# Joins of a group's banks at set times inside the next group, and four pairs by seven products in attention's output

## The chip, the cores and the metric

The kernel runs on one core of a Trainium2 chip. The metric is the device time of one execution in microseconds, as the median of several executions. A profiled execution of the same kernel gives the trace; its time and its span are listed below.

## The reference

One layer of a hybrid decoder trunk is computed in float32 for 256 tokens and a model width of 2048. Cut to what matters:

```python
h = rmsnorm(x, g_mix)
x_r, g_r, q, k, v, gate_r, gate_a = split(h @ w_in)
y_r = (gelu(g_r) * rg_lru(conv1d(x_r), w_rg_a, ..., lru_lambda)) @ w_rnn_out
q, k = head_rmsnorm(q), head_rmsnorm(k)          # 16 heads of 128
y_a = stick_breaking_attention(q, k, v) @ w_attn_out
mix = sigmoid(gate_r) * y_r + sigmoid(gate_a) * y_a
x = x + mix @ w_o
g, u = split(rmsnorm(x, g_ffn) @ w_ffn_gu)
x = x + (silu(g) * u) @ w_ffn_down
ple_gate = sigmoid(rmsnorm(x, g_ple) @ w_ple_gate)
out = x + ple_gate * (p @ w_ple_proj)
```

Nearly all of the work is in the matrix products with the weights, and each weight is read once.

## The kernel before

**Numbers in two parts.** Every operand of a product is kept as a high and a low part of reduced precision, and a product is three matmuls: high by high, high by low, low by high. In `prod` they are lines L645, L646 and L647, each 128 x 128 by 128 x 512.

**The stream of weights.** Weights come in chunks of 128 x 1024. SP's queue loads them (L284), 512 KB each, into tiles `w` or, where sums of weights are needed, `Q`. A split then makes the two parts: ScalarE copies the high part (`whi`, L373) and VectorE subtracts it (`wlo`, L374). The class `Stream` issues the splits four chunks ahead of the products (`need`), and sums two chunks further.

**Seven products for eight.** Most stages are run by `group`. A group makes four blocks of output, two blocks of 128 tokens by two halves of columns of 512. Two k-tiles taken as a pair form a 2 by 2 product that a Winograd scheme makes in seven products instead of eight. For this the weights are combined: VectorE adds (`summed`, L295), and GpSimd issues DMAs that accumulate a second weight chunk onto a tile in SBUF (`joins`, L333). The activations are combined once per pair by `half_sums`. A list of slots says in which order chunks are used: `FIRST3` and `EVEN3` have three pairs and ten plain k-tiles, `EVEN4` and `LONG` have four pairs, `TWELVE` has two pairs. `FOUR` names the stages with four pairs; `pairs_of` reads it.

**Banks.** PSUM has a pool of eight banks (`pps`). A group accumulates into six of them, named B, 5, 2, 4, 3 and 8 after their part in the scheme. B and 5 are copied out by ScalarE during the group. When the group has ended, `whole` adds each of the other four to a copied tile on VectorE: these four adds are the joins, `tt(c, q, c, ALU.add)` (L453, `H<-ps`). They give their banks back to the pool. `wo`, `dn` and `pg` have joins of their own, which add a bank onto the residual stream (`x1`) or to the gate.

**Order.** The stages are, in order: recurrent gates and branch, then `ro`, `v`, `qk` (two groups each), dense blocks of q, k and gates with attention in steps between them (`step`), `ao` (attention's output), `wo`, `gu` 0 to 3, `dn0`, `gu` 4 to 7, `dn1`, `gu` 8 to 10, `dn2`, `pg`. There are 28 places where one group follows another. The order of instructions on each engine is planned by the scheduler of the Tile framework, which simulates a timeline; `tc.issue_after` adds constraints. `behind_splits` makes what is issued in it stand behind the last split's two instructions.

Work on a group's results that is not the join itself (multiplying by a gate, the heads' norms, silu) goes to a list `todo`, of which one item is run at the start of each slot of the next group or each step of a block. Pieces that transpose results on TensorE for the next stage are in `pend`; one is run at each of the slots in `TURNED_AT`, if `todo` gave nothing to that slot. `squares` makes the sums of squares for the norms with ScalarE, `token_scales` the scales from them.

Of the kernel before, what the change touches and what calls it, by code (L numbers as in the profile page):

```python
# [39 lines left out]
TWELVE = [("S", 1, 0), ("S", 1, 1), 4, ("S", 2, 0), 5, ("S", 2, 1), 6, ("S", 3, 0), 7, ("S", 3, 1), 8, ("S", 4, 0), 9,  # L40
          ("S", 4, 1), 10, 11]
TWO = (0, 1)
FOUR = ("gu", "v", "ro", "qk")
LAST_GROUP = ("pg", 1)
W_BUFS = 4
RAW_AHEAD = 12.0
SUMS_AHEAD = 2
TURNED_AT = {"first": (5, 7, 9, 11), "twelve": (4, 6, 8, 10), "even": (9, 11, 13, 15)}
NEG = -1e30

# [116 lines left out]
def tail():  # L167


    def wide(name, w, slots, c=0):  # L170
        return [(name, g, w, c + 8 * g, c + 8 * g + 4, slots[g]) for g in range(2)]

    def blocks(*cs):
        return [("blk", b, None, c, None, None) for c, b in cs]

    def gu(*gs):
        return [("gu", g, "gu", 4 * g, 44 + 4 * g, EVEN4 if g else FIRST3) for g in gs]

    def dn(q):
        k, p = FQ0[q], FQ0[q] // 2  # L180
        slots = [x + k if isinstance(x, int) else (*x[:2], x[2] + p) if isinstance(x, tuple) else x
                 for x in (EVEN3 if FQ[q] == 16 else TWELVE)]
        return wide(f"dn{q}", "dn", [slots] * 2)

    x = [("x", 0), ("x", 1)]
    return (wide("ro", "ro", [LONG] * 2) + wide("v", "in", [EVEN4] * 2, C_V)
            + [("qk", b, "in", C_Q + 4 * b, C_K + 4 * b, EVEN4) for b in range(2)]
            + blocks(*[(c, b) for b in (2, 3) for c in (C_Q, C_K)], *[(C_GTA, b) for b in range(4)])
            + wide("ao", "ao", [EVEN3] * 2) + wide("wo", "wo", [FIRST3, EVEN3]) + gu(0, 1, 2, 3) + dn(0) + gu(4, 5, 6, 7) + dn(1)
            + gu(8, 9, 10) + dn(2)  # L190
            + wide("pg", "pg", [FIRST3[:-4] + x + FIRST3[-4:]] * 2))

# [3 lines left out]
PLAN = plan()  # L196
# [229 lines left out]
def tile_hybrid_block(ctx: ExitStack, tc: tile.TileContext, xT: bass.AP, x: bass.AP, pT: bass.AP,  # L426
# [209 lines left out]

    pend, todo = [], []

    def tok(pairs, k, t):
        x = rhs(pairs, k)  # L640
        return x[:, t * P:t * P + P], x[:, 256 + t * P:384 + t * P]
# [67 lines left out]
    def group(at, pairs, sums, after=None, also=()):  # L709
# [19 lines left out]
        for i, (_, (b, y, _, _), e, _) in enumerate(seq):  # L729
            first.setdefault(b, i)  # L730
            last[b, e] = i
            if y in ("11", "T1", "T2", "T3"):
                last[y] = i
        banks, tile_, got = {}, {}, {}
        for i, (n, (b, y, p, c), e0, e1) in enumerate(seq):
            if n not in got:
                if n in also:
                    also[n]()
                if n and todo:
                    todo.pop(0)()  # L740
                elif n in turned_at and pend:
                    with tc.issue_after(mm_.ins):
                        pend.pop(0)()
                got[n] = S_.take(("tok", name, g, slots[n]))
# [186 lines left out]

    def whole(at, pairs, sums, also=()):

        (q2, q4, q3, q8), t = group(at, pairs, sums, None, also)
        cs = [t[y] for y in ("11", "T3", "T2", "T1")]
        for c, q in zip(cs, (q2, q4, q3, q8)):
            tt(c, q, c, ALU.add)
        return cs

    def parts_sums(pairs, sums, p):  # L940
# [14 lines left out]
    for g in range(2):  # L955
        also = {n - 4 + i: (lambda p: lambda: parts_sums(xg, xsum, p))(p) for i, p in enumerate(pairs_of("v"))} if g else {
            8: last_gate, 12: next_table}
        for i, c in enumerate(whole(("ro", g), y, ysum, also)):
            o = gtr[2 * g + i // 2][i % 2]
            todo.append((lambda o, c: lambda: tt(o, c, o, ALU.mult))(o, c))  # L960
    mix_r = gtr

    vs, vc = [], []
# [131 lines left out]
            at.setdefault(ATT_FROM[hp] + f, []).append(((att_z, att_e, att_o)[d], hp))  # L1095
    osum = {}
    for i, p in enumerate(pairs_of("ao")):
        at.setdefault(61 + i, []).append((lambda p: parts_sums(ost, osum, p), p))
    slot = [0]

    def step():
        if todo:
            todo.pop(0)()
        for f, hp in at.pop(slot[0], ()):
            f(hp)
        slot[0] += 1


    for b in range(2):
        cs = whole(("qk", b), xg, xsum, {17: lambda: att_t(0), 19: lambda: att_t(1)} if b else {  # L1110
            3 + 2 * i: next_v for i in range(4)})
        for c0, c in ((C_Q, cs[:2]), (C_K, cs[2:])):
            todo.append((lambda c0, b, c: lambda: head_norms(c0, b, c, c))(c0, b, c))
    for b in (2, 3):
        for c0 in (C_Q, C_K):
            head_norms(c0, b, block(c0, b, step))
# [30 lines left out]
    for g in range(2):  # L1147
        for i, o in enumerate(whole(("ao", g), ost, osum)):
            def join(o=o, c=gta[2 * g + i // 2][i % 2], m=mix_r[2 * g + i // 2][i % 2]):
                tt(c, o, c, ALU.mult)  # L1150
                tt(c, c, m, ALU.add)

            todo.append(join)
        pend.extend(next_mix(p) for p in range(4 * g, 4 * g + 4))

    x1 = [[None] * 4 for _ in range(2)]
# [2 lines left out]
    def onto_x1(g):  # L1159

        def run(tiles):
            for n, c in enumerate(("11", "T3", "T2", "T1")):
                o = x1[n % 2][2 * g + n // 2]
                tt(o, o, tiles[c], ALU.add)
        return run

    def squares(i, t, b):
        q = tl("T")
# [38 lines left out]
    for g in range(2):  # L1207
# [2 lines left out]
                x1[t][b] = tl("C")  # L1210
                nc.sync.dma_start(x1[t][b], x[t * P:t * P + P, b * 512:b * 512 + 512])

        for n, ps in enumerate(group(("wo", g), mix, msum, onto_x1(g))[0]):
            t, b = n % 2, 2 * g + n // 2
            tt(x1[t][b], ps, x1[t][b], ALU.add)
            squares(0, t, b)
        for p in range(4 * g, 4 * g + 4):
            pend.append(next_h(hg, hsum, p, PC_GF))

# [2 lines left out]
    summed = [p for q in range(3) for p in pairs_of(f"dn{q}")]  # L1222

    def gu(g):
        also = {10: lambda: token_scales(0, rs1)} if g == 0 else {}
        c11, c21, c12, c22 = whole(("gu", g), hg, hsum, also)
        def gated(c, s_, t):
            def run():
# [1 line left out]
                stt(c, c, rs1[:, t:t + 1], s_, ALU.mult, ALU.mult)  # L1230
            return run

        todo.extend([gated(c12, c11, 0), gated(c22, c21, 1)])

        def turn(f):
            def run():
# [16 lines left out]
        pend.extend(turn(f) for f in range(2))  # L1253

    def down(q, g):
        for n, ps in enumerate(group((f"dn{q}", g), acts, asum, onto_x1(g))[0]):
            t, b = n % 2, 2 * g + n // 2
            tt(x1[t][b], ps, x1[t][b], ALU.add)
            if q == 2:
                squares(1, t, b)  # L1260
        if q == 2:
            for p in range(4 * g, 4 * g + 4):
                pend.append(next_h(h3, sum3, p, PC_GP))
# [27 lines left out]

    for g in range(2):
        qs_, t_ = group(("pg", g), h3, sum3, also={len(FIRST3) - 4: embedded(g)} | (
            {} if g else {10: lambda: token_scales(1, rs2)}))
        for n, (q, c) in enumerate(zip(qs_, ("11", "T3", "T2", "T1"))):
            t, b, op = n % 2, 2 * g + n // 2, ALU.add
            c, ps, o = t_[c], pp.pop(0), tl("T")
            ends = t_["ends"] if n == 3 else []
            if ends:
                tt(c, q, c, op)  # L1300
            for i in range(0, 512, 256 if ends else 512):
                s = slice(i, i + 256 if ends else i + 512)
                if ends:
                    tt(o[:, s], ends.pop(0)[:, s], c[:, s], ALU.add)
                else:
                    tt(o, q, c, op)
                actv(o[:, s], o[:, s], AF.Sigmoid, scale=rs2[:, t:t + 1])
                tt(o[:, s], ps[:, s], o[:, s], ALU.mult)
                tt(o[:, s], o[:, s], x1[t][b][:, s], ALU.add)
                nc.sync.dma_start(out[t * P:t * P + P, b * 512 + s.start:b * 512 + s.stop], o[:, s])  # L1310
    assert S_.pos == len(PLAN)


def _pack_weights(np, mats):
# [59 lines left out]
```

## Time and profile before

| | |
|---|---|
| median of three runs | 1852.34 us (1851.96 to 1852.41) |
| the profiled execution's own time | 1853.49 us |
| its span | 1851.8 us |
| granted TensorE clock | 0.999 |
| PE, VectorE, ScalarE, GpSimd busy | 1840.3, 1535.0, 1272.1, 128.9 us |
| moved by DMA | 414.37 MB, mean 224 GB/s |

The span is the stretch of the profiled execution from its first to its last instruction. Busy time counts an instruction from its start to its end; several matmuls are in flight at once and their ends are modelled, so the busy time of PE counts some waiting as work. In a row of the timeline stand the start, the duration, the engine, line and operation, output and inputs, shapes and the count; in brackets, idle time of the engine before it and what ended it. PE is TensorE, DVE VectorE, ACT ScalarE, POOL GpSimd and SP the queue of loads.

### The profile page before, as it was taken

What the parts mean: (1) busy time and instruction counts of PE and PEld (TensorE: products, weight loads), DVE (VectorE), ACT (ScalarE), POOL (GpSimd) and SP (SyncE); (2) the same over time, 40 slices, a digit from 0 to 9 for tenths busy, and PEclk for the clock granted to TensorE, in tenths of its full rate; (3) what the DMA queues carried; (4) which work ended last, traced back from release to release, by engine and by line L of the source; (5) the groups of instructions that cost most, each with busy time, mean ns of one, the idle gap of its engine ahead of it and who ended that gap; (6) DMA issues with size and microseconds to landing.
All of it is one profiled execution on the core that took longest, in us unless ns stands there. A gap on an engine that the chain in (4) does not pass through costs nothing.

```text
span 1851.8 us, 24810 instructions
## 1 busy us (share of the span) xinstructions
PE 1840.3 (99%) x8855; PEld 1545.9 (83%) x8855; DVE 1535.0 (83%) x1940; ACT 1272.1 (69%) x1705; POOL 128.9 (7%) x156
## 2 busy tenths in 40 slices
PE   9999999999999999999999999999999999999998
PEld 7899899888878888888888888888888888888787
DVE  7688888677898887667799889888799887898986
ACT  7687888775566777777666676665576655665774
POOL 0000000011011100000000011100111100111000
PEclk9999999999999999999999999999999999999999
DMA  8456555588788854456777788877888888887774
GB/s 294 177 177 189 184 196 194 200 251 255 234 250 243 245 178 161 143 169 217 233 247 241 220 258 242 249 246 247 252 257 256 230 242 239 259 253 234 204 239 142
DMA packets 123388, 414.37 MB, mean 224 GB/s; under 512 B 13824, under 2 KB 14464, under 8 KB 123264
## 3 DMA queue, kind: packets, MB, share of 16 engines
q1 hardware_dynamic: 101808, 359.82, 54.7%
q0 software_dynamic: 21312, 52.96, 16.7%
q8 instruction: 69, 1.13, 0.2%
q14 instruction: 55, 0.45, 0.1%
q10 hardware_dynamic: 144, 0.01, 0.0%
HBM read 410.64 MB, written 2.10 MB: 223 GB/s over the span
## 4 chain that ended last, share of the span: by engine, by line
PE 96%; DVE 2%; DMA 1%; issue 0%; ACT 0%; SPq 0%; ACTq 0%; DVEq 0%
PE ps L645 26%; PE ps L646 26%; PE ps L647 26%; PE ps L575 9%; PE ps L579 5%; PE ps L558 1%; PE ps L559 1%; PE ps L557 1%; DVE wlo L374 1%; DVE H L453 1%; PE ps L1242 1%; DVE Q L295 0%; ACT whi L373 0%; PE ps L1185 0%; PE ps L1005 0%
## 5 line engine op out<-in xcount | busy, mean ns | idle before, releaser
L646 PE MATMUL ps<-wlo,Q 128*128 128x512 f32 x2175 | 848.5, 390 | 0.8 <-DVE wlo L374 0.8
L647 PE MATMUL ps<-whi,Q 128*128 128x512 f32 x2175 | 846.0, 389 | 0.0
L645 PE MATMUL ps<-whi,Q 128*128 128x512 f32 x2175 | 753.5, 391 | 3.0 <-ACT whi L373 2.5
L374 DVE TENSOR_TENSOR wlo<-w,whi 128x1024 fp32r<-128x1024 f32 (+2 forms) x478 | 574.0, 1206 | 167.9 <-ACT whi L373 163.5
L373 ACT ACTIVATE whi<-w 128x1024 fp32r<-128x1024 f32 (+2 forms) x478 | 497.0, 1046 | 223.0 <-PE ps L647 173.4
L373 ACT ACTIVATE whi<-Q 128x1024 fp32r<-128x1024 f32 (+1 forms) x377 | 376.4, 1004 | 212.6 <-PE ps L647 182.9
L645 PEld LDWEIGHTS ps<-whi,Q 128*128 128x128 f32 x2175 | 406.9, 188 | 88.8 <-ACT whi L373 5.7
L646 PEld LDWEIGHTS ps<-wlo,Q 128*128 128x128 f32 x2175 | 408.5, 188 | 85.7 <-DVE wlo L374 2.8
L374 DVE TENSOR_TENSOR wlo<-Q,whi 128x1024 fp32r<-128x1024 f32 (+1 forms) x377 | 431.1, 1152 | 58.0 <-ACT whi L373 54.1
L647 PEld LDWEIGHTS ps<-whi,Q 128*128 128x128 f32 x2175 | 408.4, 188 | 84.3
L333 POOL DMA_DIRECT2D Q<-in_w_dram x148 | 126.8, 859 | 1674.9 <-DVE Q L295 583.2
L575 PE MATMUL ps<-Q,whi 128*128 128x512 f32 x704 | 170.7, 392 | 0.0
L575 PEld LDWEIGHTS ps<-Q,whi 128*128 128x128 f32 x704 | 128.7, 188 | 24.5
L295 DVE TENSOR_TENSOR Q<-Q,Q 128x512 f32<-128x512 f32 (+1 forms) x148 | 128.2, 878 | 15.0 <-DMA Q<-in_w_dram 14.3
L459 ACT ACTIVATE H<-ps 128x512 f32<-128x512 f32 (+1 forms) x179 | 93.9, 538 | 52.7 <-PE ps L647 43.3
L453 DVE TENSOR_TENSOR H<-H,H 128x512 f32<-128x512 f32 (+2 forms) x214 | 119.8, 570 | 2.5 <-ACT H L459 1.9
L453 DVE TENSOR_TENSOR H<-ps,H 128x512 f32<-128x512 f32 (+1 forms) x162 | 93.3, 605 | 16.8 <-PE ps L647 12.0
L579 PEld LDWEIGHTS ps<-Q,wlo 128*128 128x128 f32 x704 | 90.4, 191 | 3.5
L579 PE MATMUL ps<-Q,wlo 128*128 128x256 f32 x704 | 91.5, 283 | 0.0
L459 ACT ACTIVATE Q<-H 128x512 fp32r<-128x512 f32 x70 | 43.0, 625 | 38.6 <-DVE H L453 38.0
L459 ACT ACT_TABLE_LOAD x52 | 66.7, 1283 | 3.3 <-DVE Q L453 2.5
L453 DVE TENSOR_TENSOR Q<-H,Q 128x512 fp32r<-128x512 f32 (+1 forms) x78 | 52.9, 682 | 0.8 <-ACT Q L459 0.7
(125 smaller groups left out, 890.3 us busy)
## 6 DMA issues: line engine op xcount, KB each, us to landing
w<-in_w_dram SPq DMA_DIRECT2D x453, 512.0 KB, 4.2
Q<-in_w_dram SPq DMA_DIRECT2D x202, 512.0 KB, 6.0
Q<-in_w_dram POOLq DMA_DIRECT2D x54, 512.0 KB, 6.9
Q<-in_w_dram POOLq DMA_DIRECT2D x94, 256.0 KB, 5.1
w<-in_w_dram SPq DMA_DIRECT2D x16, 448.0 KB, 3.3
H<-in_x_dram SPq DMA_DIRECT2D x8, 256.0 KB, 7.2
H<-in_xT_dram SPq DMA_DIRECT2D x7, 256.0 KB, 5.6
out_dram<-H SPq DMA_DIRECT2D x7, 256.0 KB, 2.9
```

The lines of the kernel that those rows point to most:

```text
L295: add = lambda o, a, b: self.nc.vector.tensor_tensor(o, a, b, ALU.add)
L333: self.nc.gpsimd.dma_start(t[:, c:], src[:, a:a + 1024 - c], accum_op=ALU.add)
L373: self.hi_ins = self.nc.scalar.activation(h[:, q], t[:, q], AF.Copy)
L374: self.lo_ins = self.nc.vector.tensor_tensor(l[:, q], t[:, q], h[:, q].bitcast(F32), ALU.subtract)
L453: nc.vector.tensor_tensor(o, a, b, op)
L459: nc.scalar.activation(o, i, f, **kw)
L557: nc.tensor.matmul(o, wt[0], xh, start=start, stop=False)
L575: nc.tensor.matmul(pss[e], wt[0], rhs(xs, k), start=(k == 0), stop=(k == n - 1))
L579: nc.tensor.matmul(pss[e][:, :256], wt[1], rhs(xs, k)[:, :256], start=False, stop=False)
L645: nc.tensor.matmul(ps, x[0], wh, start=start, stop=False, skip_group_check=goes_on)
L646: nc.tensor.matmul(ps, x[0], wl, start=False, stop=False, skip_group_check=goes_on)
L647: return nc.tensor.matmul(ps, x[1], wh, start=False, stop=stop, skip_group_check=goes_on)
```

## The change

1. `JOINS_AT = (0, 1.3, 2.7, 4.0)` gives the four joins of `whole` a time in microseconds from the start of the next group. `later_on` puts them in `todo` with their time; `run_todo`, called at each slot, issues all that are due, each inside `behind_splits`. A slot's time is 0.68 us times the products before it. In a block's `step` the time is 2.7 us times the step's number.
2. Work on the joined results gets times of its own in the same way: the product with the gate after `ro` from 8 us, the join with the mix after `ao` from 2.7, the norms of heads after `qk` at 5.4 and 8.1, silu after `gu` at 5.4 and 8.1. The joins of `wo`, `dn0` to `dn2` and of `pg`'s first group get `JOINS_AT`, and their `squares` or `finish` (sigmoid, product, sum, store) 6.8 + 2.7n. `token_scales` moves from slot 10 to slot 13.
3. A piece of `pend` is run from its slot on only when no join is left in `todo`.
4. `ao` joins `FOUR`: its lists become `EVEN4` with four pairs, and one more pair gets half-sums ahead of it, from step 60 in place of 61.

Counted over the program, matmul instructions on PE go from 8853 to 8847, and VectorE has 14 instructions more.

```diff
-FOUR = ("gu", "v", "ro", "qk")
+FOUR = ("gu", "v", "ro", "qk", "ao")
+JOINS_AT = (0.0, 1.3, 2.7, 4.0)
...
-            + wide("ao", "ao", [EVEN3] * 2) + wide("wo", "wo", [FIRST3, EVEN3]) + gu(0, 1, 2, 3) + dn(0) + gu(4, 5, 6, 7) + dn(1)
+            + wide("ao", "ao", [EVEN4] * 2) + wide("wo", "wo", [FIRST3, EVEN3]) + gu(0, 1, 2, 3) + dn(0) + gu(4, 5, 6, 7) + dn(1)
...
+    def later_on(at, f, first=True):
+
+        todo.append((at, f, first))
+
+    def run_todo(t):
+        due = [x for x in todo if x[0] <= t]
+        todo[:] = [x for x in todo if x[0] > t]
+        for _, f, _ in due:
+            with behind_splits():
+                f()
...
+        begin = [0.0]
+        for x in slots:
+            begin.append(begin[-1] + 0.68 * len(products(x)))
+        turns = list(turned_at)
...
-                if n and todo:
-                    todo.pop(0)()
-                elif n in turned_at and pend:
+                run_todo(begin[n])
+                if pend and turns and n >= turns[0] and not any(x[2] for x in todo):
+                    turns.pop(0)
                     with tc.issue_after(mm_.ins):
                         pend.pop(0)()
...
-        (q2, q4, q3, q8), t = group(at, pairs, sums, None, also)
+        qs_, t = group(at, pairs, sums, None, also)
         cs = [t[y] for y in ("11", "T3", "T2", "T1")]
-        for c, q in zip(cs, (q2, q4, q3, q8)):
-            tt(c, q, c, ALU.add)
+        for a, c, q in zip(JOINS_AT, cs, qs_):
+            later_on(a, (lambda c, q: lambda: tt(c, q, c, ALU.add))(c, q))
...
-            todo.append((lambda o, c: lambda: tt(o, c, o, ALU.mult))(o, c))
+            later_on(8 + 2.7 * i, (lambda o, c: lambda: tt(o, c, o, ALU.mult))(o, c))
...
-        at.setdefault(61 + i, []).append((lambda p: parts_sums(ost, osum, p), p))
+        at.setdefault(60 + i, []).append((lambda p: parts_sums(ost, osum, p), p))
...
-        if todo:
-            todo.pop(0)()
+        run_todo(2.7 * slot[0])
...
-        for c0, c in ((C_Q, cs[:2]), (C_K, cs[2:])):
-            todo.append((lambda c0, b, c: lambda: head_norms(c0, b, c, c))(c0, b, c))
+        for a, c0, c in ((5.4, C_Q, cs[:2]), (8.1, C_K, cs[2:])):
+            later_on(a, (lambda c0, b, c: lambda: head_norms(c0, b, c, c))(c0, b, c))
...
-            todo.append(join)
+            later_on(2.7 + 1.36 * i, join)
...
+    def ends_x1(pss, g, i):
+
+        for n, ps in enumerate(pss):
+            t, b = n % 2, 2 * g + n // 2
+            later_on(JOINS_AT[n], (lambda o, ps: lambda: tt(o, ps, o, ALU.add))(x1[t][b], ps))
+            if i is not None:
+                later_on(6.8 + 2.7 * n, (lambda t, b: lambda: squares(i, t, b))(t, b), False)
...
-        for n, ps in enumerate(group(("wo", g), mix, msum, onto_x1(g))[0]):
-            t, b = n % 2, 2 * g + n // 2
-            tt(x1[t][b], ps, x1[t][b], ALU.add)
-            squares(0, t, b)
+        ends_x1(group(("wo", g), mix, msum, onto_x1(g))[0], g, 0)
...
-        also = {10: lambda: token_scales(0, rs1)} if g == 0 else {}
+        also = {13: lambda: token_scales(0, rs1)} if g == 0 else {}
...
-        todo.extend([gated(c12, c11, 0), gated(c22, c21, 1)])
+        later_on(5.4, gated(c12, c11, 0))
+        later_on(8.1, gated(c22, c21, 1))
...
-            tt(x1[t][b], ps, x1[t][b], ALU.add)
-            if q == 2:
-                squares(1, t, b)
+        ends_x1(group((f"dn{q}", g), acts, asum, onto_x1(g))[0], g, 1 if q == 2 else None)
...
+            if g == 0:
+                later_on(JOINS_AT[n], (lambda c, q: lambda: tt(c, q, c, ALU.add))(c, q))
+                later_on(6.8 + 2.7 * n, finish)
+                continue
```

More of the change, by code (lines that the diff above doesn't have):

```diff
@@ L1293, in tile_hybrid_block, with finish @@
         qs_, t_ = group(("pg", g), h3, sum3, also={len(FIRST3) - 4: embedded(g)} | (
-            {} if g else {10: lambda: token_scales(1, rs2)}))
+            {} if g else {13: lambda: token_scales(1, rs2)}))
         for n, (q, c) in enumerate(zip(qs_, ("11", "T3", "T2", "T1"))):
[L1296 to L1306, printed above, removed]
+            t, b, c, ps = n % 2, 2 * g + n // 2, t_[c], pp.pop(0)
+            def finish(s=slice(0, 512), t=t, b=b, o=c, ps=ps):
                 actv(o[:, s], o[:, s], AF.Sigmoid, scale=rs2[:, t:t + 1])
@@ L1310, in tile_hybrid_block @@
                 nc.sync.dma_start(out[t * P:t * P + P, b * 512 + s.start:b * 512 + s.stop], o[:, s])
-    assert S_.pos == len(PLAN)
+            if g == 0:
+                later_on(JOINS_AT[n], (lambda c, q: lambda: tt(c, q, c, ALU.add))(c, q))
+                later_on(6.8 + 2.7 * n, finish)
+                continue
+            tt(c, q, c, ALU.add)
+            if n < 3:
+                finish()
+            for i, ps_ in enumerate(t_["ends"] if n == 3 else []):
+                s = slice(256 * i, 256 * i + 256)
+                tt(c[:, s], ps_[:, s], c[:, s], ALU.add)
+                finish(s)
+    assert S_.pos == len(PLAN) and not todo and not pend
 def _pack_weights(np, mats):
```

2 lines of the change are left out of this document (removed).

## The prediction

> **What bounds the kernel now.** I read the page first (busy shares, then the chain that ended last).
>
> ```profile
> span 1851.8 us, 24810 instructions
> ## 1 busy us (share of the span) xinstructions
> PE 1840.3 (99%) x8855; PEld 1545.9 (83%) x8855; DVE 1535.0 (83%) x1940; ACT 1272.1 (69%) x1705; POOL 128.9 (7%) x156
> ...
> PE 96%; DVE 2%; DMA 1%; issue 0%; ACT 0%; SPq 0%; ACTq 0%; DVEq 0%
> ```
>
> TensorE carries 96% of the chain and VectorE, busy 83% of the span, is next. So there are two ways to a shorter time: fewer matmuls, or less waiting of PE. The waits of PE say how much waiting the profile itself counts:
>
> ```profile
> PE ps L645 <- ACT whi L373: 2.5, 7, 0.6
> PE ps L494 <- DVE H L491: 1.6, 1, 1.6
> PE ps L646 <- DVE wlo L374: 0.8, 3, 0.4
> ```
>
> L494 is the start of the kernel. What is left is 3.3 us, all of it for the two halves of a split. That is too little, because the end of a matmul is modelled. The timeline of PE shows it:
>
> ```profile
> 510.96 1.52 PE L645 MATMUL ps<-whi,Q 128*128 128x512 f32 x6
> ...
> 515.52 0.39 PE L647 MATMUL ps<-whi,Q 128*128 128x512 f32 x1
> 516.14 0.50 PE L646 MATMUL ps<-wlo,Q 128*128 128x512 f32 x1 [0.23 <-DVE wlo L374]
> ```
>
> A matmul is drawn 0.39 us long, but six in a row take 1.52, so they start every (1.52 − 0.39) / 5 = 0.226 us. From 515.52 to 516.14 is 0.62: 0.39 is lost there, and the row says 0.23. I therefore count matmuls in windows. The first row here is an undisturbed stretch (columns: stretch, length, busy time and count of each engine, granted clock, share of the DMA engines, GB/s); five disturbed ones follow, and the last two are attention's output.
>
> ```profile
> 500.00:513.00 13.00, 13.00 (x59) 10.74 (x58) 10.96 (x16) 5.68 (x7) 2.55 (x3) 1.00 0.93 264
> 513.00:520.00 7.00, 6.01 (x23) 3.75 (x22) 6.95 (x8) 3.22 (x4) 1.40 (x2) 1.00 0.79 152
> 601.00:603.00 2.00, 1.57 (x7) 0.99 (x6) 2.00 (x2) 1.73 (x2) 0.50 (x1) 1.00 0.06 11
> 1061.00:1064.00 3.00, 2.78 (x12) 1.86 (x11) 2.85 (x3) 1.25 (x3) 0.85 (x1) 1.00 0.89 225
> 1066.00:1068.50 2.50, 2.13 (x10) 1.35 (x9) 2.33 (x3) 2.50 (x5) 0.75 (x1) 1.00 0.74 248
> 1753.00:1758.00 5.00, 4.30 (x17) 2.63 (x16) 4.95 (x5) 3.65 (x5) 0.87 (x2) 1.00 0.88 149
> 885.00:925.00 40.00, 40.00 (x178) 33.14 (x177) 30.46 (x30) 23.48 (x26) 3.42 (x4) 1.00 0.76 234
> 925.00:967.00 42.00, 42.00 (x195) 34.73 (x194) 40.44 (x57) 28.28 (x35) 3.43 (x4) 1.00 0.79 253
> ```
>
> 13 us at 0.226 are 57.5 starts; 59 are listed, as matmuls at the edges count too, so a clean window holds T / 0.226 + 1.5. By that 513 to 520 should hold 32.5 and has 23: 9.5 × 0.226 = 2.15 us lost. Likewise 3.4 missing (0.76) at 601, 2.8 (0.63) at 1061, 2.6 (0.58) at 1066 and 6.6 (1.50) at 1753. The sum is **5.6 us**, give or take one matmul in each window, some 0.5 in all. All five stand just behind a change of stage, ro to v, v to qk, wo to gu, dn2 to pg, and in all five DVE is at 93% or more. The queue of DVE at these places:
>
> ```profile
> 504.24 0.69 DVE L295 TENSOR_TENSOR Q<-Q,Q 128x512 f32<-128x512 f32 x1 [2.04 <-DMA Q<-in_w_dram]
> 504.85 0.68 DVE L453 TENSOR_TENSOR H<-ps,H 128x512 f32<-128x512 f32 x1
> ...
> 508.99 0.68 DVE L453 TENSOR_TENSOR H<-ps,H 128x512 f32<-128x512 f32 x1
> ...
> 514.87 1.22 DVE L374 TENSOR_TENSOR wlo<-Q,whi 128x1024 fp32r<-128x1024 f32 x1
> 516.00 1.82 DVE L295 TENSOR_TENSOR Q<-Q,Q 128x512 f32<-128x512 f32 x2
> ```
> ```profile
> 597.01 2.73 DVE L456 SCALAR_TENSOR_TENSOR Q<-H,rstd_tok,Q 128x512 fp32r<-128x512 f32 x4
> 599.66 1.22 DVE L295 TENSOR_TENSOR Q<-Q,Q 128x1024 f32<-128x1024 f32 x1
> 600.80 1.22 DVE L374 TENSOR_TENSOR wlo<-Q,whi 128x1024 fp32r<-128x1024 f32 x1
> ```
> ```profile
> 1052.61 2.05 DVE L453 TENSOR_TENSOR H<-ps,H 128x512 f32<-128x512 f32 x3 [0.66 <-PE ps L647]
> ```
> ```profile
> 1750.45 1.28 DVE L453 TENSOR_TENSOR H<-ps,H 128x512 f32<-128x512 f32 x2
> 1751.65 0.68 DVE L295 TENSOR_TENSOR Q<-Q,Q 128x512 f32<-128x512 f32 x1
> 1752.24 0.68 DVE L453 TENSOR_TENSOR Q<-H,Q 128x512 fp32r<-128x512 f32 x1
> 1752.85 1.22 DVE L374 TENSOR_TENSOR wlo<-Q,whi 128x1024 fp32r<-128x1024 f32 x1
> ```
>
> DVE does these one behind the other, and a split that the next group's first products need stands behind joins of the last group (H<-ps) and work on their results (L456). Three joins take 2.05 and two 1.28, so one adds some 0.65 to 0.68 to what stands behind it; a group leaves four, 2.7 us.
>
> **The change, part by part.**
>
> *Times of the joins.* Nothing leaves DVE here; four joins a group move from one batch at the group's end to 0, 1.3, 2.7 and 4.0 us of the next group, each issued behind the last split issued by then. By the program order of the changed kernel the DVE work ahead of the splits at a group's start is 0.6 to 3.6 us less at every boundary between groups. Place by place, at 0.6 for an instruction of 512 in a row of them (two take 1.28, one 0.68): at ro to v the split behind 514.87 loses three joins and a product ahead of it and the next ones four pieces, 2.4 us against 2.15 lost. At v to qk two of the four L456 go behind the split of 600.80, 1.3 against 0.76. At wo to gu three joins of 2.05 and their squares on ACT go, against 0.63 and 0.58. At dn2 to pg two joins of 1.28 and the two that stood just before go, against 1.50. The add at 504.24 waited 2.04 for its DMA, which the change does not touch; it stands ahead of the joins in both orders. Each cover is larger than its loss, the one at dn2 to pg if at least half of what leaves counts. I take all five as gone: −5.6. What is late next at these places is ACT's half of the split (L373) and the landing of raw weights; both would take part of it back (second rival).
>
> *What a moved join holds up.* A join empties a bank of PSUM, and the next group uses six of eight. Four banks are left with the old results, so the fifth bank of the new group, which its list asks for behind seven products (7 × 3 × 0.226 = 4.7 us; five and 3.4 us in ro), must come from the first join, and the sixth, at 5.4 us or later, from the second. The first is due at 0 and the second at 1.3, each perhaps behind a split of 1.22 and 0.7 long: done by about 2 and by 3.5 to 4 us. No wait, with 1.4 to 2.7 us of cover; if that is gone, PE waits at up to 28 boundaries (first rival). The third and fourth bank are for transposes, whose slots begin at 6.8 us or later.
>
> *Work on the results.* Products with gates, norms, squares and silu move to 2.7 to 15 us of the next group. The same instructions, later, behind splits: 0. Their readers are transposing pieces, which now wait until no join is left, and a scale that moves three slots back with the squares. The joins are due by 6.8 us at the latest, about the first piece's slot: 0, and if a piece slips a slot, matmuls of that slot go ahead of it.
>
> *Stores and loads on SP's queue.* pg's first four stores go from the group's end into group 1, and SP waits for their data with weight loads behind them; x1's loads stand a little earlier.
>
> ```profile
> H<-in_x_dram SPq DMA_DIRECT2D x8, 256.0 KB, 7.2
> ...
> out_dram<-H SPq DMA_DIRECT2D x7, 256.0 KB, 2.9
> ```
>
> If a store holds the queue until its data come, the loads behind it are late; I bound that by one whole landing, 2.9 us, in pg alone, and below by 0, since the stores waited in the same queue before. The loads are due 12 us ahead by the code, so I take 0.
>
> *Attention's output by four pairs.* Eight products of one pair of k-tiles become seven in each of two groups: by the program order 8853 matmul instructions become 8847, 6 × 0.226 = 1.4 us off PE, and PE sets the end there: 885 to 967 shows no loss. By the Trainium skill, page "TensorE: Matmul & The Clock Gate", section "Back-to-back issue gap", a 128x512 matmul in a stream of weight loads and matmuls comes every 131 ns or so, by which the six would be 0.8 us; these rows show 226, at a granted clock of 1.00, and the row decides.
>
> For it DVE gets per group one split of 1024 and one of 512 more and two adds of 512 (L295). At what each adds to a row of work, 1.13 (from 599.66 to 600.80) and 0.60 (from 1751.65 to 1752.24), that is 1.13 + 0.60 + 1.20 = 2.9 us. It also gets half-sums of a fourth pair, one add and one subtract of 512 and four of 128, between 1.2 and 3.6 us by the same 0.60, in the blocks ahead of the groups, where no row of the PE waits lies: 0. The first group has room: DVE is busy 30.46 of 40. The second has not: 40.44 of 42, and with 2.9 more in 0.7 less (three matmuls) it is 43.3 in 41.3, over by 2.0. Between the ends of 0 (DVE works ahead by as much as the four splits issued early, and part of the rows there belongs to wo's preparation, which can slide) and 2.0 I take 1.0, the middle, since neither is nearer. POOL gets four more accumulating DMAs on an engine at 7%: 0.
>
> *Sum.* −5.6 − 1.4 + 1.0 = −6.0 on the profiled execution of 1853.49 (its span is 1851.8, so 1.7 lie around it): 1847.5, span 1845.8. That execution is 1.15 above the median, 1852.34. On the median: **1846.3**.
>
> **The rivals.**
>
> *First, slower: the banks.* If the delayed joins come later than estimated (behind a split that itself waits for ACT, or for a raw weight as at 504.24 with 2.04), the fifth bank isn't free and PE stops at each of 28 boundaries. The gain of 7.0 is gone from 7.0 / 28 = 0.25 us a boundary; one half of a split's 1.22, 0.6, would give 28 × 0.6 = 16.8 − 6.0 = +10.8, so 1863. Against it speak the cover, and that the list of PE's waits names no join (H<-ps) now, though the joins of ro's second group ran from 504.85 to 508.99 between other work. The Trainium skill, page "PSUM — Partial Sum Buffer", section "Summary: rules for kernel authors", says "Evacuate promptly", which this change does not do. No wait for a bank stands in this trace, so the rule has no number here.
>
> *Second, about the same: another wait takes the place.* Where DVE is at 93 to 100%, PE gets its split earlier only if the data and ACT are there. For it speaks that most of PE's waits, 2.5 of 3.3, are put down to ACT's half. If half of the 5.6 stays, and attention costs its full 2.0, it is −2.8 − 1.4 + 2.0 = −2.2: 1850.1. If two thirds go, −3.7 − 1.4 + 1.5: 1848.7.
>
> *Third: it changes nothing.* The planner could have placed the joins there anyway. The order of the changed kernel's instructions says no; if it were so, −1.4 + 1.0: 1851.9.
>
> **How the numbers follow.** The forecast has 0.71, the second rival 0.20, the banks 0.07, the third 0.02. 0.2%, 3.7 us, is about what a measurement of this kernel can tell from no change, so "same" reaches from 1848.6 to 1856.0. Of the second rival a tenth comes out faster than that: faster 0.73, same 0.20, slower 0.07. Range: below, all stalls with the counting error (−6.1), no price for attention (−1.4): 1844.8; above, the second rival's 1850.1. What is left out is the banks, the third rival and some of the second.
>
> **What would show it.** Right: counts of 31 or more per 7 us at ro to v and the like; joins between splits, none in a batch, at group starts; 8847 matmuls; PE waits under 1 us. The attention term: matmuls starting over 0.3 us apart in the second ao group. Wrong: a PE wait on a join (DVE H) at the eighth product of groups, or the same waits for L373 and L374 at the same five places.

## The result, and the profile after

| | before | after |
|---|---|---|
| median of 16 runs each | 1852.43 us | 1856.82 us |
| lowest and highest | 1851.66 to 1853.94 | 1855.46 to 1858.47 |
| the profiled execution, its span | 1853.49, 1851.8 | 1855.46, 1853.8 |

The ratio is 1.0022 with a 95% interval of 1.0015 to 1.003: the change made the kernel 0.22% slower, where 1846.3 was forecast. The two profiled executions differ by 2.0 us only, since that of before lies 1.1 above its median and that of after 1.4 below. The traces can therefore account for 2.0 of the 4.4 us; the other 2.4 lie between executions, which one trace of each kernel can't show. Nine of the changed kernel's 16 executions list a granted clock of 0.998 and seven 0.999, and 0.001 over the whole span would be 1.9 us, as an estimate; but at 0.999 there are times from 1855.46 up to 1857.69.

The page and the list of PE's waits after:

```profile
PE 1839.0 (99%) x8849; PEld 1546.0 (83%) x8849; DVE 1542.4 (83%) x1954; ACT 1275.8 (69%) x1710; POOL 133.1 (7%) x160
```
```profile
PE ps L659 <- DVE Q L454: 2.6, 1, 2.6
PE ps L657 <- ACT whi L374: 2.2, 3, 1.1
PE ps L495 <- DVE H L492: 1.6, 1, 1.6
PE ps L657 <- DVE Q L454: 1.2, 1, 1.2
PE ps L657 <- DVE H L454: 0.5, 1, 0.5
```

PE has the six matmuls less, and a new wait of 2.6 us, the longest in the list. (Lines have moved: L657 to L659 are the three matmuls of a product, L374 and L375 the split, L296 the sums, L454 joins and other two-operand work on VectorE, L460 what ScalarE copies and squares.) The last row is new as well, and it is a wait for a join of attention's output:

```profile
972.52 0.69 DVE L454 TENSOR_TENSOR H<-ps,H 128x512 f32<-128x512 f32 x1
```
```profile
973.26 0.50 PE L657 MATMUL ps<-whi,Q 128*128 128x512 f32 x1 [0.53 <-DVE H L454]
```

The matmul doesn't read H, so what it waited for is the bank that this join gives back. That is the first rival's wait, seen once.

The windows after, for ro to v, v to qk, the two at wo to gu, dn2 to pg, the two groups of attention's output, and wo's start:

```profile
513.00:520.00 7.00, 7.00 (x32) 5.80 (x31) 7.00 (x9) 5.65 (x7) 1.72 (x2) 1.00 0.70 145
598.00:600.00 2.00, 2.00 (x10) 1.67 (x9) 2.00 (x4) 1.39 (x3) 0.86 (x1) 1.00 0.03 8
1060.00:1063.00 3.00, 3.00 (x15) 2.49 (x14) 1.81 (x3) 2.28 (x3) 0.06 (x1) 1.00 0.99 246
1065.00:1067.50 2.50, 2.50 (x13) 2.07 (x12) 1.29 (x2) 1.33 (x2) 0.00 (x0) 1.00 0.98 252
1755.00:1760.00 5.00, 4.06 (x17) 3.12 (x18) 5.00 (x6) 2.05 (x3) 0.86 (x1) 1.00 0.50 73
883.00:922.00 39.00, 39.00 (x174) 32.30 (x173) 33.06 (x34) 24.85 (x29) 6.89 (x8) 1.00 0.89 264
922.00:965.00 43.00, 43.00 (x199) 35.52 (x198) 41.83 (x59) 28.25 (x36) 2.59 (x3) 1.00 0.83 245
965.00:995.00 30.00, 25.13 (x112) 18.70 (x110) 29.23 (x37) 18.69 (x23) 3.44 (x4) 1.00 0.77 188
```

The first four hold 32, 10, 15 and 13 matmuls, as many as a clean window does: what was lost there before (4.1 us) is gone. The fifth still has 17 in 5 us, as before. The last is new: 112 matmuls where the same 30 us of wo's start held 142 before:

```profile
967.00:997.00 30.00, 30.00 (x142) 24.72 (x141) 30.00 (x38) 18.93 (x23) 1.71 (x2) 1.00 0.60 169
```

30 × 0.226 = 6.8 us lost. −4.1 − 1.4 + 6.8 = +1.3 of the 2.0. Most of the other 0.7 stands in the blocks behind qk, where a wait of PE for VectorE grew from 0.54 us, in the first row here, to 1.17:

```profile
699.39 0.50 PE L645 MATMUL ps<-whi,Q 128*128 128x512 f32 x1 [0.54 <-DVE Q L453]
```
```profile
696.88 0.50 PE L657 MATMUL ps<-whi,Q 128*128 128x512 f32 x1 [1.17 <-DVE Q L454]
```

The row of before at wo's start says a second thing, which the prediction had not looked at: VectorE was busy 30.00 of 30.00 us at wo's start already, without PE losing anything.

How ro to v went well is seen in VectorE's timeline after. Splits come between the joins, where 504.85 to 508.99 held four joins against one split before:

```profile
507.86 1.22 DVE L375 TENSOR_TENSOR wlo<-Q,whi 128x1024 fp32r<-128x1024 f32 x1
509.00 0.69 DVE L454 TENSOR_TENSOR H<-ps,H 128x512 f32<-128x512 f32 x1
509.60 1.22 DVE L375 TENSOR_TENSOR wlo<-w,whi 128x1024 fp32r<-128x1024 f32 x1
510.73 0.69 DVE L454 TENSOR_TENSOR H<-ps,H 128x512 f32<-128x512 f32 x1
```

And the wait of 2.6, on VectorE, ScalarE and PE:

```profile
987.67 0.70 DVE L454 TENSOR_TENSOR Q<-Q,H 128x512 f32<-128x512 f32 x1
988.27 1.23 DVE L375 TENSOR_TENSOR wlo<-w,whi 128x1024 fp32r<-128x1024 f32 x1
989.41 1.23 DVE L375 TENSOR_TENSOR wlo<-Q,whi 128x1024 fp32r<-128x1024 f32 x1
990.54 0.70 DVE L454 TENSOR_TENSOR H<-H,H 128x512 f32<-128x512 f32 x1
991.15 1.30 DVE L454 TENSOR_TENSOR Q<-ps,Q 128x512 fp32r<-128x512 f32 x2
```
```profile
989.01 1.09 ACT L460 ACTIVATE Q<-ps 128x512 fp32r<-128x512 f32 x2 [0.94 <-PE ps L1151]
```
```profile
991.90 1.20 PE L659 MATMUL ps<-whi,Q 128*128 128x512 f32 x4 [2.60 <-DVE Q L454]
```

The last sum with the mix (Q<-Q,H) ends at 988.4. Pieces are transposed, ScalarE makes their high part from 989.01, and the low part stands in VectorE's queue behind splits that nobody waits for yet, and comes at 991.15. The product of k-tile 8 waits for it. These 2.6 us are less than half of the 6.8: ahead of them PE waits 1.13 at 969.81 for ScalarE's half of a split, 0.53 for the join, and 0.47 at 981.41 for VectorE's half.

### The profile page after: what moved, and what is told of

Same layout as the page of the kernel before. It is cut to its first block, busy times and chain, and to the rows that moved or that the text cites. A ratio compares the mean times of both kernels' runs of the same rounds, so it can differ in the third digit from the quotient of the medians.

```text
span 1853.8 us, 24812 instructions
## 1 busy us (share of the span) xinstructions
PE 1839.0 (99%) x8849; PEld 1546.0 (83%) x8849; DVE 1542.4 (83%) x1954; ACT 1275.8 (69%) x1710; POOL 133.1 (7%) x160
## 3 DMA queue, kind: packets, MB, share of 16 engines
q8 instruction: 69, 1.13, 0.2%
## 4 chain that ended last, share of the span: by engine, by line
PE 97%; DVE 2%; ACT 1%; issue 0%; DMA 0%; SPq 0%; DVEq 0%; ACTq 0%
PE ps L657 26%; PE ps L659 26%; PE ps L658 26%; PE ps L576 9%; PE ps L580 5%; PE ps L559 1%; PE ps L560 1%; PE ps L558 1%; DVE wlo L375 1%; DVE H L454 1%; PE ps L1263 1%; PE ps L1208 0%; PE ps L1021 0%; DMA H<-in_x_dram 0%; DVE Q L454 0%
## 5 line engine op out<-in xcount | busy, mean ns | idle before, releaser
L659 PE MATMUL ps<-whi,Q 128*128 128x512 f32 x2173 | 843.2, 389 | 2.6 <-DVE Q L454 2.6
L657 PE MATMUL ps<-whi,Q 128*128 128x512 f32 x2173 | 752.3, 392 | 4.0 <-ACT whi L374 2.2
L375 DVE TENSOR_TENSOR wlo<-w,whi 128x1024 fp32r<-128x1024 f32 (+2 forms) x474 | 570.5, 1208 | 163.4 <-ACT whi L374 159.1
L374 ACT ACTIVATE whi<-w 128x1024 fp32r<-128x1024 f32 (+2 forms) x474 | 493.8, 1048 | 216.9 <-PE ps L659 166.3
L374 ACT ACTIVATE whi<-Q 128x1024 fp32r<-128x1024 f32 (+1 forms) x385 | 384.8, 1005 | 212.4 <-PE ps L659 177.9
L375 DVE TENSOR_TENSOR wlo<-Q,whi 128x1024 fp32r<-128x1024 f32 (+1 forms) x385 | 441.5, 1155 | 61.8 <-ACT whi L374 58.0
L657 PEld LDWEIGHTS ps<-whi,Q 128*128 128x128 f32 x2173 | 407.5, 188 | 89.2 <-ACT whi L374 3.3
L659 PEld LDWEIGHTS ps<-whi,Q 128*128 128x128 f32 x2173 | 408.0, 188 | 87.2 <-DVE Q L454 2.8
L334 POOL DMA_DIRECT2D Q<-in_w_dram x152 | 130.6, 866 | 1669.9 <-PE ps L659 623.1
L296 DVE TENSOR_TENSOR Q<-Q,Q 128x512 f32<-128x512 f32 (+1 forms) x152 | 130.6, 877 | 15.1 <-DMA Q<-in_w_dram 14.7
L460 ACT ACTIVATE H<-ps 128x512 f32<-128x512 f32 (+1 forms) x179 | 94.2, 540 | 61.1 <-PE ps L659 51.0
L454 DVE TENSOR_TENSOR H<-H,H 128x512 f32<-128x512 f32 (+1 forms) x216 | 121.0, 571 | 4.9 <-ACT H L460 4.3
L454 DVE TENSOR_TENSOR H<-ps,H 128x512 f32<-128x512 f32 (+1 forms) x162 | 97.2, 610 | 9.5 <-PE ps L659 5.1
L460 ACT ACTIVATE Q<-H 128x512 fp32r<-128x512 f32 x71 | 43.8, 626 | 37.5 <-DVE H L454 36.9
L454 DVE TENSOR_TENSOR Q<-H,Q 128x512 fp32r<-128x512 f32 (+1 forms) x79 | 53.9, 688 | 3.0 <-ACT Q L460 2.9
```

The lines of the kernel that those rows point to most:

```text
L296: add = lambda o, a, b: self.nc.vector.tensor_tensor(o, a, b, ALU.add)
L334: self.nc.gpsimd.dma_start(t[:, c:], src[:, a:a + 1024 - c], accum_op=ALU.add)
L374: self.hi_ins = self.nc.scalar.activation(h[:, q], t[:, q], AF.Copy)
L375: self.lo_ins = self.nc.vector.tensor_tensor(l[:, q], t[:, q], h[:, q].bitcast(F32), ALU.subtract)
L454: nc.vector.tensor_tensor(o, a, b, op)
L460: nc.scalar.activation(o, i, f, **kw)
```

## The experiments

Each was timed in five rounds, with 4 to 11 executions in all. The ratio stands against the kernel before on the same chip, whose medians were 1852.34, 1851.93 and 1852.14 in the three sets of four. Two theories stood at the start. Theory A: the fourth pair's work on VectorE has no room from the second group into wo. Theory B: the moved joins and mix hold up wo's transposing pieces, and the fourth pair alone is harmless.

**The two parts of the change, crossed.** First, the kernel before with four pairs alone:

```diff
-FOUR = ("gu", "v", "ro", "qk")
+FOUR = ("gu", "v", "ro", "qk", "ao")
...
-... wide("ao", "ao", [EVEN3] * 2) ...
+... wide("ao", "ao", [EVEN4] * 2) ...
...
-        at.setdefault(61 + i, []) ...
+        at.setdefault(60 + i, []) ...
```

> The kernel before with attention's output alone changed to four pairs by seven products (times of joins as before). Theory A (the 2.9 us per group that the fourth pair adds on VectorE has no room, since VectorE is 97 to 99% busy from the second group on and through wo's start, so PE waits at wo's start): 4 to 7 us slower than before, 1856 to 1859, with PE losing 5 to 8 us between 965 and 1000. Theory B (the moved joins and products with the mix hold up wo's first transposes; the fourth pair itself is harmless): 1.4 us faster to no change, 1851 to 1852.5, no loss of over 1 us there.

Measured: 1858.02, ratio 1.0029 (1.0018 to 1.0041), 5.7 us slower. PE has 118 matmuls in the 30 us of wo's start, so 24 × 0.226 = 5.4 us are lost. The six executions range from 1855.65 to 1859.44; the traced one took 1856.01, so the 5.4 belong to 3.7 us against the kernel before and not to 5.7. Nearly all of them are two waits for a split:

```profile
974.13 0.73 PE L645 MATMUL ps<-whi,Q 128*128 128x512 f32 x2 [2.13 <-ACT whi L373]
...
978.26 0.50 PE L646 MATMUL ps<-wlo,Q 128*128 128x512 f32 x1 [1.98 <-DVE wlo L374]
```

VectorE makes no split from 970.41 to 976.97; it works on attention's results and on sums of weights. In the order of the kernel before the fourth pair costs 5.4 us by itself. Theory B as it stood has fallen.

The same three lines undone in the changed kernel:

> The changed kernel with attention's output back at three pairs (times of joins as changed). Theory A: faster than before by what left at ro to v, v to qk and wo to gu, some 4 us: 1848, no loss at wo's start. Theory B: the loss of some 7 us at wo's start stays, 1856 to 1858.

Measured: 1851.44, ratio 0.9996 (0.9987 to 1.0005). 135 matmuls at wo's start: 1.6 us lost, with a wait of 0.86 on a piece's low part. The times of joins alone save little, for they lose at attention's output a part of what they save elsewhere; neither theory had that.

Then the changed kernel with attention's output joined at once (with `now=True`, `whole` issues the four adds itself):

```diff
-        for i, o in enumerate(whole(("ao", g), ost, osum)):
+        for i, o in enumerate(whole(("ao", g), ost, osum, now=True)):
...
-            later_on(2.7 + 1.36 * i, join)
+            later_on((1.3, 2.7, 5.4, 6.8)[i], join)
```

> The changed kernel, four pairs kept, but attention's output has its four joins at once at the group's end, and the product with the gate and the sum with the mix one in each of the next group's first four slots, as before. Theory A: still 4 to 7 us lost at wo's start, 1854 to 1857. Theory B: that loss goes, 1848 to 1850.

Measured: 1850.48, ratio 0.9992 (0.9983 to 1.0001); 133 matmuls, 2.0 us lost. Theory A had said that 4 to 7 stay. So the order of the work on attention's output decides how dear the fourth pair is: 6.8 us in the changed kernel, 2.0 here, and 5.4 in the kernel before, which joined at once too. What sets this run apart from that one at wo's start is that product and sum are issued behind splits (by `later_on`, so not quite "as before") and that pieces wait for the list of joins; no run tests these two apart.

With three pairs as well:

> Both of the last two: three pairs, and attention's output joined as before, the other stages as changed. Theory A: like the run with three pairs alone within 1 us, 1848. Theory B: 1848, some 8 us less than with three pairs alone.

Measured: 1849.78, ratio 0.9988 (0.9979 to 0.9997). 142 matmuls: nothing lost. What wo's start loses in the four cases, all of them versions of the changed kernel:

| | joined at once | joined at the new times |
|---|---|---|
| three pairs | 0 | 1.6 us |
| four pairs | 2.0 us | 6.8 us |

In this table the two together cost more than their sum, 3.6. Counted from the kernel before they do not: four pairs alone lose 5.4 there, the new times alone 1.6, and both 6.8. So the excess belongs to the order in the left column, with its work behind splits, and not to the two parts of the change as such. What both ways of counting leave is that the one part puts more work on VectorE and the other puts work that is needed early further back in its queue. The next runs test each.

**The amount of work.** To the last run, five instructions in each of attention's two groups:

```diff
+        def extra(m=mix_r[3][1]):
+            with behind_splits():
+                tt(m, m, m, ALU.max)
...
-        ... whole(("ao", g), ost, osum, now=True)
+        ... whole(("ao", g), ost, osum, {n: extra for n in (2, 5, 8, 11, 14)}, now=True)
```

> Three pairs in attention's output, joined at once (the fastest run so far, 1849.8), with five more VectorE instructions of 128x512 in each of its two groups (a tile's maximum with itself): 3.0 us a group, about what the fourth pair adds, and nothing for PE, GpSimd or the loads. Theory A (amount of work on VectorE: it has no room from the second group into wo): PE loses some 2 us at wo's start as with four pairs, 1851 to 1853. Theory B (the fourth pair's own chain, GpSimd's DMA, sum, split, is what comes late): no loss, 1849.5 to 1850.3.

Measured: 1851.23, ratio 0.9996 (0.9988 to 1.0005), 1.5 us more than without. Its row at wo's start, and that of the run without:

```profile
965.00:995.00 30.00, 29.68 (x135) 23.39 (x134) 29.95 (x38) 17.80 (x22) 2.58 (x3) 1.00 0.70 188
```
```profile
965.00:995.00 30.00, 30.00 (x142) 24.80 (x141) 29.35 (x37) 18.88 (x23) 1.71 (x2) 1.00 0.69 191
```

Seven matmuls, 1.6 us, are lost, nearly as with four pairs (2.0), though nothing was added for GpSimd, the loads or the splits. In this order, then, VectorE's time alone makes most of the fourth pair's price. The other way round, the changed kernel with less of it:

```diff
                 tt(c, o, c, ALU.mult)
-                tt(c, c, m, ALU.add)
```

> The changed kernel without the sum of the two branches (the add of the recurrent branch to attention's in the join after attention's output is left out, so the mix is attention's alone): eight VectorE instructions of 128x512 less, 2.4 us a group, behind the second group in wo's first slots. Theory A: the 6.9 us lost at wo's start shrink by 2.4 or more, 1852 to 1854.5. Theory B: they stay, 1856 to 1857.

Measured: 1848.94, ratio 0.9985 (0.9976 to 0.9994), 140 matmuls: 0.5 us lost instead of 6.8. The shrinkage, 6.3, is more than the 4.8 us taken out in both groups together. The edit also shortens the way to the pieces; this run can't tell that from the smaller amount.

Four pairs only where there is room:

```diff
-... wide("ao", "ao", [EVEN4] * 2) ...
+... wide("ao", "ao", [EVEN4, EVEN3]) ...
```

> Four pairs in the first group of attention's output alone, three in the second, joined at once. Theory A: VectorE has room in the first group (33 of 39 us busy with four pairs), so 0.7 us of matmuls goes and little or nothing is lost at wo's start: 1848.8 to 1849.8. Theory B: half of the loss that four pairs had, 1 us: 1850.

Measured: 1849.72, ratio 0.9987 (0.9979 to 0.9996); 139 matmuls, 0.7 us lost. That is what the three matmuls saved, so it came to nothing, at the upper end of what theory A expected.

**The order of work.** The changed kernel with product and sum at each join's own time:

```diff
-            later_on(2.7 + 1.36 * i, join)
+            later_on(JOINS_AT[i], join)
```

> The changed kernel, four pairs, with the product and the sum behind each join of attention's output at the join's own time (0, 1.3, 2.7, 4.0) in place of 2.7 + 1.36 n. Theory C (late mix: the transposed pieces' low parts come too late for the product of k-tile 8, the wait of 2.6 us): that wait shrinks by 1 to 2.7, 1853.5 to 1855.5. Rival (VectorE's total alone): 1856 to 1857.

Measured: 1853.89, ratio 1.001 (1.0001 to 1.0018): 2.9 us below the changed kernel's median, 2.6 when each is taken against the kernel before of its own set. The wait on the piece shrinks from 2.60 to 0.86:

```profile
990.61 1.19 PE L659 MATMUL ps<-whi,Q 128*128 128x512 f32 x4 [0.86 <-DVE Q L454]
```

119 matmuls at wo's start, 5.2 us lost: 1.6 less than in the changed kernel, which is what the wait gave back. Summing earlier thus gives back about a quarter of the 6.8. The waits ahead of it are as they were, 1.12 for ScalarE's half of a split and 0.53 for a join.

And joined at once, but with product and sum put off:

```diff
-            later_on((1.3, 2.7, 5.4, 6.8)[i], join)
+            later_on(2.7 + 2.7 * i, join)
```

> The run with four pairs and joins at once (1850.5), with the product and the sum behind each join at 2.7, 5.4, 8.1 and 10.8 us instead of 1.3 to 6.8. Theory C (late mix): a wait of PE on a piece's low part of 2 to 4 us appears at the product of k-tile 8, 1852.5 to 1854.5. Rival (only the joins themselves being late costs): 1850 to 1851.

Measured: 1853.07, ratio 1.0008 (0.9999 to 1.0017), 2.6 us worse than with early sums (2.8 against the kernel before of each set). 123 matmuls, 4.3 us lost. The wait appears, though smaller than expected, and the rest is splits that come late, the longest of them first here:

```profile
970.69 0.50 PE L658 MATMUL ps<-wlo,Q 128*128 128x512 f32 x1 [1.13 <-DVE wlo L375]
...
989.40 1.19 PE L659 MATMUL ps<-whi,Q 128*128 128x512 f32 x4 [0.86 <-DVE Q L454]
```

Late work on the results costs, then; it is not the joins alone.

**dn2 to pg.** Pieces of the groups of twelve k-tiles a slot earlier, in the run with three pairs joined at once:

```diff
-TURNED_AT = {..., "twelve": (4, 6, 8, 10), ...}
+TURNED_AT = {..., "twelve": (3, 5, 7, 9), ...}
```

> Three pairs, joined at once, and the transposing pieces of the groups of twelve k-tiles (dn2) a slot earlier. At dn2 to pg VectorE stood 2.16 us for the high part of the last half-sums, which ScalarE did behind a copy that waited 4.92 us for PE. Theory A2 (that order is the cause of the loss there): 1.5 us less, 1848.3. Rival: ScalarE's copy is ahead of it again, 1849.8.

Measured: **1848.09**, ratio 0.998 (0.9971 to 0.9989), 3.8 us below the kernel before in the same set, and the fastest of all. In the run it was made from, ScalarE and VectorE had this:

```profile
1746.41 0.60 ACT L460 ACTIVATE H<-ps 128x512 f32<-128x512 f32 x1 [4.92 <-PE ps L659]
1746.91 0.62 ACT L460 ACTIVATE Q<-H 128x512 fp32r<-128x512 f32 x1
```
```profile
1747.56 0.69 DVE L454 TENSOR_TENSOR Q<-H,Q 128x512 fp32r<-128x512 f32 x1 [2.16 <-ACT Q L460]
```

ScalarE's high part of the last half-sums (Q<-H) stood behind a copy of a bank that PE had not finished, and VectorE's queue stood behind that. The changed kernel has the same (2.16 at 1753.58). The kernel before has not: there the high part came first, and VectorE's low part, at 1752.24 in the prediction's rows, followed without a wait:

```profile
1748.33 0.62 ACT L459 ACTIVATE Q<-H 128x512 fp32r<-128x512 f32 x1
...
1752.84 0.57 ACT L459 ACTIVATE H<-ps 128x512 f32<-128x512 f32 x1
```

So this wait came with the change. With the pieces a slot earlier the high part goes ahead of the copy again, and VectorE does not wait:

```profile
1740.03 0.61 ACT L460 ACTIVATE Q<-H 128x512 fp32r<-128x512 f32 x1
```
```profile
1744.73 0.69 DVE L454 TENSOR_TENSOR Q<-H,Q 128x512 fp32r<-128x512 f32 x1
```

Between 1747 and 1757 there are 48 matmuls against 40 before the edit, 1.8 us.

**The rival of the prediction, priced.** The fastest run with every due time 3 us later:

```diff
-        due = [x for x in todo if x[0] <= t]
+        due = [x for x in todo if x[0] + 3.0 <= t]
```

> The fastest version so far (three pairs, attention's output joined at once, pieces of dn2 a slot earlier, 1848.1) with every due time 3 us later, so joins at 3.0, 4.3, 5.7 and 7.0 us of the next group. It puts a price on the rival of the prediction, banks held too long. If a group's fifth bank is needed at 4.7 us and the first join ends near 5, PE loses 0.3 to 1.5 us at most boundaries, some 27 of them: 1856 to 1880, with waits of PE on the joins (DVE H, L454). If the joins are still in time: 1847.5 to 1849, no such waits.

This kernel reads one tile of v ahead of its join. Measured: 1870.72, ratio 1.0101 (1.0088 to 1.0115). The time is within the range that the banks were to give, but the banks didn't give it. The longest waits of PE between 690 and 1080 are on results and on a split:

```profile
PE ps L1024 <- DVE H L454: 2.8, 1, 2.8
PE ps L658 <- DVE wlo L375: 1.2, 2, 0.8
PE ps L1154 <- DVE Q L454: 1.0, 1, 1.0
```

L1024 transposes normed heads and L1154 the mix. From 1100 to 1690, fourteen changes of group in gu, dn0 and dn1, PE has no wait at all and as many matmuls as without the shift (2641 there):

```profile
1100.00:1690.00 590.00, 590.00 (x2643) 488.68 (x2642) 515.23 (x576) 375.22 (x430) 66.72 (x78) 1.00 0.83 247
```

Compared start by start with the run it was made from, PE is 12 us behind by 1090, no more than that by 1690, and falls back by 12 more behind 1700, 10 of them where gu gives way to dn2 (1700 to 1725) and dn2 to pg (1760 to 1795). No wait there is for a join either; the two longest rows are these:

```profile
PE ps L657 <- ACT whi L374: 3.0, 3, 2.1
PE ps L659 <- DVE Q L454: 2.1, 1, 2.1
...
```

A part of the time is the clock's: from 700.5, 994.1, 1717.7 and 1768.9, close behind waits of PE, the granted clock is 0.5 for 3.4 us. That costs half of these 13.6 us, 6.8 of the 22.6, as an estimate. One of the four stretches, with 8 matmuls where a clean window of 3 us holds 14.8:

```profile
1718.00:1721.00 3.00, 3.00 (x8) 2.32 (x8) 2.42 (x4) 1.83 (x2) 0.86 (x1) 0.50 0.59 147
```

**A way out that failed.** Four pairs, joined at once, with dn2's earlier pieces, and the sum with the mix on GpSimd:

```diff
-                tt(c, c, m, ALU.add)
+                nc.gpsimd.tensor_tensor(c, c, m, ALU.add)
```

> Four pairs in both groups of attention's output, joined at once, pieces of dn2 a slot earlier, and the sum of the two branches (eight adds of 128x512) on GpSimd instead of VectorE: 2.4 us a group less on VectorE where it is full. Theory A (amount of work on VectorE): nothing over 0.3 us is lost at wo's start, and the 1.4 us of matmuls come off: 1846.5 to 1847.3. Rival (GpSimd's adds are slower than 0.7 us or hold up the accumulating DMAs queued behind them, and the mix comes late): 1848 to 1851 with a wait on the pieces.

Measured: 1858.53, ratio 1.0035 (1.0022 to 1.0047). The rival's reason, at a far higher price than it gave. GpSimd's first sum, one of its later ones, and a VectorE instruction beside that:

```profile
928.59 13.06 POOL L1169 TENSOR_TENSOR Q<-Q,H 128x512 f32<-128x512 f32 x1 [7.33 <-DVE Q L454]
```
```profile
982.36 2.21 POOL L1169 TENSOR_TENSOR Q<-Q,H 128x512 f32<-128x512 f32 x1 [0.63 <-DVE Q L454]
```
```profile
983.33 1.77 DVE L454 TENSOR_TENSOR Q<-H,Q 128x512 f32<-128x512 f32 x1
```
```profile
941.71 0.48 PE L1154 MATMUL ps<-ident,Q 128*128 128x128 f32 x1 [4.20 <-POOL Q L1169]
```

## Why the prediction was wrong

**Right: the stalls behind ro, v and wo, and the six matmuls.** 4.1 of the 5.6 us went, in the four windows behind these stages, with the joins standing between splits. ACT's half and the landings did not take them back there.

**Wrong: dn2 to pg, −1.50 forecast, nothing measured.** The joins did leave VectorE's queue there, but another wait took their place, as the second rival had it: in the changed kernel VectorE stands 2.16 us for ScalarE's high part of the last half-sums, which stands behind a copy that waits for PE. In the kernel before ScalarE had the two the other way round. Moving the pieces by a slot, in the run with three pairs, turned the order back and gave 1.8 us by count. Why the planner changed it, no run shows.

**The step that failed: "Between the ends of 0 ... and 2.0 I take 1.0".** The term for attention's four pairs, +1.0, measured 6.8 us in the changed kernel and 5.4 alone. The size of the extra work, 2.9 us a group, was near enough: 3.0 us of other work cost 1.6 us where the fourth pair cost 2.0. What was wrong is the reason that part of it could slide into wo. The prediction's windows ended at 967, and the 30 us behind had VectorE busy 30.00 of 30.00, so an overflow was not given back there. The sign that was named, starts over 0.3 us apart in the second group of attention's output, does not come: PE is busy 43.00 of 43.00 there, and the loss lies wholly behind it. Nor is the price an amount alone. That the upper end of the term, 2.0, was met in one run is luck, for the same work cost 5.4 and 6.8 in two other orders.

**And "The same instructions, later, behind splits: 0".** That holds where VectorE has room, as in gu and dn, where the shift by 3 us cost nothing. At wo's start it does not: the joins' sums are the inputs of pieces whose low parts go through the same full queue, and the product of k-tile 8 needs them. The prediction named the readers and compared the due times of the joins with the slot of the first piece; it should have gone on to the time at which VectorE, behind its splits, could make the piece's low part. In the runs the new times lose 1.6 us at wo's start with three pairs, and with four an earlier sum gives 1.6 back. What is left of the 6.8 is mostly splits that come late themselves.

**Overlooked: a wait behind qk.** PE's waits before have a fourth row, `PE ps L645 <- DVE Q L453: 0.5, 1, 0.5`, which the prediction left out when it put the list at 3.3 us, all for splits. It is the wait in the blocks behind qk, for a result and not for a split, and it grew by 0.6. It stands at 1.15 with three pairs as well, so it goes with the new times. With it the sum comes out: −4.1 − 1.4 + 6.8 + 0.6 = +1.9 of the 2.0.

**The slower rival had the wrong mechanism.** Kept banks cost one wait of 0.53 us in the changed kernel, and with joins 3 us later no wait for a join is listed at all. The Trainium skill, page "PSUM — Partial Sum Buffer", section "Summary: rules for kernel authors", asks to evacuate promptly; in gu and dn no wait bears it out here. Six of the eight banks are in use at once there, and by the prediction's count the fifth is asked for 4.7 us into a group. What did make the kernel slower, a full VectorE that reaches past the window, was inside the forecast as a term of 1.0, and in the second rival as 2.0, but no rival was made of it.

What stays open: why the executions of the changed kernel spread over 3.0 us, and half of its loss against the median with it. The granted clock can be a part of it only.

## What to carry to other kernels

When work is added to an engine, follow its busy share past the stage that gets the work, up to the first stretch with real room; the overflow lands ahead of it, on whoever waits. When work is put off, take its reader's reader as well, and count each step through the queues that are full: here sums put off by a few us turned into a wait of 2.6 on PE, through a piece's low part. In these runs it paid to spread joins behind splits where the engine has room, and to join at once where it has none. Test the parts of a change apart, and in the order in which the work will stand: the same fourth pair cost 2.0, 5.4 and 6.8 us with three orders of the work beside it, the last with the new times' own 1.6 in it.

## What the runs showed of the hardware

An add of 128x512 took 0.68 us on VectorE. On GpSimd, whose spans are rough, it took 1.6 to 2.2, and the first one 13.06; PE stood for that one until 941.71, where it ended. Beside GpSimd's later sums three products of that size on VectorE took 1.77 to 1.79 instead of 0.68, while the splits between them kept their 1.21 and a product during the first sum its 0.68. So the move cost time on both engines. The Trainium skill, page "Perfetto Trace Analysis", section "Optimizing Scalar/DVE Operations", says that the two share a read port, so that work moved between them might not help; the 1.77 agrees with it. Around PE's waits for GpSimd (4.20 and 1.64 us) the granted clock was 0.66 between 940 and 950, where it was 1.00 in the stretches on both sides:

```profile
940.00:950.00 10.00, 6.65 (x25) 5.32 (x26) 4.10 (x5) 2.87 (x5) 7.96 (x7) 0.66 0.51 113
```

Together with the four stretches at 0.5 in the run with later due times, each close behind waits of PE that come to 1.9 to 3.3 us within 7 us, this makes PE's waits dearer than their length in these two runs. It isn't so everywhere: around the wait of 2.60 in the changed kernel's trace the granted clock is 1.00.
